# Gate and up projections of a ConvFFN by Strassen's seven products, in a hybrid decoder step on one core

## The chip, the cores and the metric

The kernel runs on one core of a Trainium2 chip. The metric is the device time of one execution in microseconds; three runs before the change took 1549.66, 1551.98 and 1552.0 us, median 1551.98. Engines are named as in the profile: PE is TensorE (matmul), PEld its weight loads, DVE is VectorE, ACT ScalarE, POOL GpSimd, SP SyncE, from which all transfers are issued.

## What is computed

The reference is one inference step of a two-layer decoder trunk for 512 prompt tokens and 8 sequences of 8 sample tokens, all in float32, with D_MODEL 1024 and D_FF 2816. Layer 0 mixes tokens by a convolution module beside windowed attention, layer 1 by a Mamba-2 mixer. After each mixer stands the part that is changed:

```python
def conv_ffn(h, hist, w_gate, w_up, conv_w, conv_b, w_down):
    gate = h @ w_gate
    padded = jnp.concatenate([hist, gate], axis=1)
    gc = causal_dwconv(padded, conv_w, conv_b)          # width 3
    y = (jax.nn.silu(gc) * (h @ w_up)) @ w_down
    return y, padded[:, -(FFN_CONV_WIDTH - 1):]
...
        fp, f1 = conv_ffn(rmsnorm(xp, norm_ffn[layer]), ...)
        xp = xp + fp
```

Here h is `x * rsqrt(mean(x^2) + eps) * g`. The last two gate rows of each sequence are outputs too.

## The kernel before

**Layout.** Activations lie transposed: channels on the 128 partitions, the 576 tokens (512 + 64) along the free axis, in two halves of 288 (`HALF`). x is eight tiles of 128x576. A projection's weights come as tiles of 128 output channels, 128x1024: eight blocks of 128x128, one for each 128 input channels.

**Three matmuls per product.** To keep float32 accuracy with the faster fp32r matmuls, each operand is split into a rounded high part and the rest. `weights` (L163, L164) does so for a weight tile (ACT copies the high part, DVE subtracts), `split` (L193, L194) for activations, and `mm3` (L173 to L175) issues high x high, high x low and low x high into one PSUM bank. A tile and half thus takes 8 x 3 = 24 matmuls of 128x288 with 24 weight loads.

**Norm.** With `early` set, as for both FFNs, `norm_tile` makes h as x times the gain as soon as a tile of x is final, and the matmuls run on that; the factor rs (one over the root of the mean square, from `rstd`, L202 to L220) is applied afterwards to the projections' sums (L329, L333, L334 for the gate, L347 for the up side). Without `early`, as for the Mamba layer (`norm_o`), `norm_half` scales h by rs first (L261) and splits it, and the matmuls wait for that.

**The FFN stage** (`ffn`). There are 22 gate and 22 up tiles of 128 channels. Three gate tiles go first (`lead`), then up tile f and gate tile f + 3 in turn. A gate tile's sums are written to `gbuf`, the history is put in front (POOL, L327, L328), the width-3 convolution runs on DVE (L339, L341 twice), SiLU on ACT (L344, L345). An up tile's sums are multiplied with that (L354) and split into a pair y. The down projection runs in three parts (`PARTS`, of 8, 7 and 7 tiles f), each as soon as its tiles are there: `out_proj` takes eight output tiles m in two halves, and `add_x` (L288) adds each sum to x on DVE. The last part of the first FFN also makes the next layer's norm.

**Order and buffers.** A scheduler at build time orders each engine's instructions by readiness in its own model, with the order of the program as priority; `keep_in_program_order` pins a matmul behind what was issued before it. On the chip each engine takes its queue in order. Raw weights have three buffers (`wr`), split ones three pairs (`wh`, `wl`). PSUM has eight banks: four in turn for projections (`mm`), four for the rest (`aux`). Other tiles come from a list of 48 + 11 slots in SBUF (`S`, `free`), first freed, first used again.

Of the kernel before, what the change touches and what calls it, by code (L numbers as in the profile page):

```python
# [23 lines left out]
PARTS = ((0, 8), (8, 15), (15, 22))  # L24
# [25 lines left out]

class Builder:
    NSLOT = 48
    EXTRA = 11

    def __init__(self, nc, tc, d, stack):
# [9 lines left out]
        self.used = {}  # L65

# [25 lines left out]
    def pm(self):  # L92
        return self.ps("mm", "mm")

# [140 lines left out]
    def norm_begin(self, gname, early):  # L235
        self.gname, self.early = gname, early
        self.ssq, self.rs = self.S("ssq"), self.S("rs")
        self.h = [self.pair("h") for _ in range(8)]
        self.hf = []
# [12 lines left out]
    def norm_half(self, half):  # L252
# [3 lines left out]
        if not self.early:  # L256
            for k in range(8):
# [5 lines left out]
                self.split(t[:, sl], self.h[k], sl)  # L263
# [3 lines left out]
    def norm_end(self):  # L267
        self.free(self.rs, self.h)
# [43 lines left out]
    def ffn(self, l, next_norm):  # L312
        nc, d = self.nc, self.d
        hist, so = self.S("fhist", NF * 16), self.S("fso", NF * 16)
# [4 lines left out]
        rs = self.rs  # L319
        bt = lambda ap: ap.rearrange("p (b t) -> p b t", t=8)  # L320

        def gate_evac(f):
            def go(half, p):
                if half == 0:
                    g = gbuf[f] = self.S("gbuf", 594)
                    gs = g[:, 514:594].rearrange("p (b c) -> p b c", c=10)
                    nc.gpsimd.memset(g[:, 0:2], 0.0)  # L327
                    nc.gpsimd.tensor_copy(gs[:, :, 0:2], hist[:, f * 16:f * 16 + 16].rearrange("p (b c) -> p b c", c=2))  # L328
                    nc.vector.tensor_tensor(g[:, 2:290], p[:, :HB], rs[:, :HB], op=MUL)  # L329
                    return  # L330
                g = gbuf.pop(f)
                gs = g[:, 514:594].rearrange("p (b c) -> p b c", c=10)
                nc.vector.tensor_tensor(g[:, 290:514], p[:, 0:224], rs[:, HB:NP], op=MUL)  # L333
                nc.vector.tensor_tensor(gs[:, :, 2:10], bt(p[:, 224:288]), bt(rs[:, NP:]), op=MUL)  # L334
                nc.gpsimd.tensor_copy(so[:, f * 16:f * 16 + 16].rearrange("p (b c) -> p b c", c=2), gs[:, :, 8:10])
                nc.gpsimd.tensor_copy(po[:, f * 2:f * 2 + 2], g[:, 512:514])  # L336
                cv = self.S("gconv", 594)
                w = lambda k: self.pv(f"fw{l}", f * 3 + k)
                nc.vector.tensor_scalar(cv[:, :592], g[:, 0:592], w(0), None, op0=MUL)  # L339
                for k in (1, 2):  # L340
                    nc.vector.scalar_tensor_tensor(cv[:, :592], g[:, k:592 + k], w(k), cv[:, :592], op0=MUL, op1=ADD)  # L341
                sl = sl_of[f] = self.S("gsilu")
                b = self.pv(f"fb{l}", f)
                nc.scalar.activation(sl[:, :NP], cv[:, :NP], AF.Silu, bias=b)  # L344
                nc.scalar.activation(bt(sl[:, NP:]), cv[:, 514:594].rearrange("p (b c) -> p b c", c=10)[:, :, 0:8],  # L345
                                     AF.Silu, bias=b)
                nc.vector.tensor_tensor(sl, sl, rs, op=MUL)  # L347
                self.free(g, cv)
            return go

        def up_evac(f):
            def go(half, p):
                sl = sl_of[f]
                nc.vector.tensor_tensor(sl[:, HALF[half]], p[:, :HB], sl[:, HALF[half]], op=MUL)  # L354
                if half == 1:
                    y_of[f] = self.pair("y")
                    self.split(sl, y_of[f])
                    self.free(sl_of.pop(f))
            return go
# [1147 lines left out]
```

## Time and profile before

| | |
|---|---|
| median of three runs | 1551.98 us (1549.66 to 1552.0) |
| span of the profiled execution | 1551.3 us |
| its time outside the span, against the median | 0.7 us |
| matmuls in the span | 11635 |
| first FFN, 217 to 630 us | 413.0 us, DVE busy 221.56, POOL 15.92 |
| second FFN, 1129.5 us to the end | 421.8 us, DVE busy 217.79, POOL 15.38 |

How to read the lines of the profile. A window's row gives from:to, its length, then the busy time of PE, PEld, DVE, ACT and POOL with the number of instructions, then the granted share of the TensorE clock, the busy share of the DMA engines and GB/s. A row of a group gives line, engine, operation, the tile written <- the tiles read, shapes and count, then busy us and the mean ns of one, then the idle time before them and what ended it. A row of one line's instructions gives the shortest, median and longest ns. A row of the timeline gives start and length in us, the instruction, how many were merged, and in brackets the idle time before it with what ended it.

### The profile page before, as it was taken

The numbers are of one execution on the slowest core, as the hardware profiler recorded it, in microseconds if no ns is written. First come the engines' busy times: TensorE is split into PE (matmuls) and PEld (weight loads), VectorE is DVE, ScalarE is ACT, GpSimd is POOL, SyncE is SP. The second block draws the span as 40 slices with busy tenths as digits, with TensorE's granted clock in tenths as the row PEclk, the third lists the DMA queues.
The fourth block names the chain that finished last, engine by engine and source line by source line (L and its number), as shares of the span: only waits on it lengthen the run. The fifth ranks groups of instructions, "written<-read, shape, count | busy, mean of one in ns | idle before, by whom it ended". The sixth has DMA issues, their size and how long they took to land.

```text
span 1551.3 us, 28549 instructions
## 1 busy us (share of the span) xinstructions
PE 1520.5 (98%) x11635; PEld 1449.8 (93%) x11635; DVE 1018.5 (66%) x1805; ACT 649.3 (42%) x1232; POOL 154.7 (10%) x365
## 2 busy tenths in 40 slices
PE   8999999999999999999999999999999999999999
PEld 7977799999999999898988988998999999999999
DVE  7969887553555464678896786777976644663552
ACT  6356553221222222486855654646632222321220
POOL 0036001000000000011211112102010000000000
PEclk9999999999999999999999999999999999999999
DMA  8515223222222222136245245245222222223222
GB/s 239 136 42 131 85 70 98 86 86 85 83 77 78 92 82 85 55 104 202 71 148 180 83 115 185 72 125 173 87 84 85 91 83 82 82 73 92 82 87 75
DMA packets 69938, 157.80 MB, mean 102 GB/s; under 512 B 19871, under 2 KB 24607, under 8 KB 69807
## 3 DMA queue, kind: packets, MB, share of 16 engines
q1 hardware_dynamic: 69806, 155.97, 33.2%
q8 instruction: 92, 1.51, 0.4%
q14 instruction: 40, 0.32, 0.1%
HBM read 140.73 MB, written 15.21 MB: 101 GB/s over the span
## 4 chain that ended last, share of the span: by engine, by line
PE 88%; DVE 5%; ACT 4%; DMA 2%; issue 1%; SPq 0%; ACTq 0%; DVEq 0%
PE mm L173 27%; PE mm L175 27%; PE mm L174 26%; DMA acb<-acd 2%; PE yp L1148 1%; DVE wl L164 1%; ACT acb L1116 1%; PE mm L594 1%; ACT wh L163 1%; PE pst L1081 1%; PE pt L1063 1%; ACT sm L661 1%; PE py L1133 1%; PE pst L1200 1%; DMA out_ssm_s<-h 1%
## 5 line engine op out<-in xcount | busy, mean ns | idle before, releaser
L173 PE MATMUL mm<-hh,wh 128*128 128x288 f32 x2272 | 677.8, 299 | 6.8 <-ACT wh L163 5.5
L174 PE MATMUL mm<-hl,wh 128*128 128x288 f32 x2272 | 673.9, 297 | 0.7 <-DVE hl L389 0.4
L175 PE MATMUL mm<-hh,wl 128*128 128x288 f32 x2272 | 673.3, 297 | 0.5 <-DVE wl L164 0.4
L163 ACT ACTIVATE wh<-wr 128x1024 fp32r<-128x1024 f32 (+2 forms) x215 | 223.3, 1039 | 544.6 <-PE mm L174 275.1
L173 PEld LDWEIGHTS mm<-hh,wh 128*128 128x128 f32 x2272 | 428.3, 189 | 16.0 <-ACT wh L163 6.0
L174 PEld LDWEIGHTS mm<-hl,wh 128*128 128x128 f32 x2272 | 429.0, 189 | 4.8 <-issue 1.8
L175 PEld LDWEIGHTS mm<-hh,wl 128*128 128x128 f32 x2272 | 428.7, 189 | 3.2 <-issue 1.4
L164 DVE TENSOR_TENSOR wl<-wr,wh 128x1024 fp32r<-128x1024 f32 (+2 forms) x215 | 258.6, 1204 | 73.0 <-ACT wh L163 71.4
L173 PE MATMUL mm<-yh,wh 128*128 128x288 f32 x960 | 285.9, 298 | 1.5 <-DVE x L288 1.4
L175 PE MATMUL mm<-yh,wl 128*128 128x288 f32 x960 | 284.2, 297 | 1.3 <-DVE wl L164 1.3
L174 PE MATMUL mm<-yl,wh 128*128 128x288 f32 x960 | 285.3, 297 | 0.0
L173 PEld LDWEIGHTS mm<-yh,wh 128*128 128x128 f32 x960 | 181.1, 189 | 5.7 <-DVE x L288 2.5
L175 PEld LDWEIGHTS mm<-yh,wl 128*128 128x128 f32 x960 | 181.1, 189 | 2.4 <-DVE wl L164 1.6
L174 PEld LDWEIGHTS mm<-yl,wh 128*128 128x128 f32 x960 | 181.2, 189 | 1.5 <-issue 1.0
L288 DVE TENSOR_TENSOR x<-x,mm 128x288 f32<-128x288 f32 x192 | 84.9, 449 | 143.0 <-PE mm L175 142.8
L333 DVE TENSOR_TENSOR gbuf<-mm,rs 128x224 f32<-128x224 f32 x44 | 17.2, 391 | 108.6 <-PE mm L175 108.6
L344 ACT ACTIVATE gsilu<-gconv,par 128x512 f32<-128x512 f32 x44 | 31.8, 724 | 115.1 <-DVE gconv L341 115.1
L341 DVE SCALAR_TENSOR_TENSOR gconv<-gbuf,par,gconv 128x592 f32<-128x592 f32 x88 | 73.1, 831 | 1.5
L354 DVE TENSOR_TENSOR gsilu<-mm,gsilu 128x288 f32<-128x288 f32 x88 | 40.0, 454 | 50.5 <-PE mm L175 50.5
L880 DVE SCALAR_TENSOR_TENSOR cconv<-cbuf,par,cconv 128x600 f32<-128x600 f32 x72 | 59.6, 838 | 10.1 <-ACT cconv L878 9.5
L336 POOL COPY fpo<-gbuf 128x2 f32<-128x2 f32 x44 | 12.4, 281 | 476.0 <-DVE gbuf L333 476.0
L1116 ACT ACTIVATE acb<-acb,ac 128x128 f32<-128x128 f32 x128 | 41.4, 390 | 35.6 <-DMA acb<-acd 25.0
(322 smaller groups left out, 1593.6 us busy)
## 6 DMA issues: line engine op xcount, KB each, us to landing
wr<-in_w_gate SPq DMA_DIRECT2D x44, 512.0 KB, 3.5
wr<-in_w_up SPq DMA_DIRECT2D x44, 512.0 KB, 3.5
wr<-in_w_in_o SPq DMA_DIRECT2D x40, 512.0 KB, 3.6
wr<-in_w_down SPq DMA_DIRECT2D x32, 448.0 KB, 3.3
wr<-in_w_down SPq DMA_DIRECT2D x16, 512.0 KB, 3.5
h<-in_h SPq DMA_DIRECT2D x32, 256.0 KB, 3.1
acb<-acd SPq DMA_DIRECT2D x32, 256.0 KB, 4.2
out_ssm_s<-h SPq DMA_DIRECT2D x32, 256.0 KB, 2.6
```

The costliest lines, as they stand in the source:

```text
L163: nc.scalar.activation(hi[:, a:b], raw[:, a:b], AF.Copy)
L164: nc.vector.tensor_tensor(lo[:, a:b], raw[:, a:b], hi[:, a:b].bitcast(F32), op=SUB)
L173: nc.tensor.matmul(out, hi[:, ws], xh[:, sl], start=i == 0, stop=False)
L174: nc.tensor.matmul(out, hi[:, ws], xl[:, sl], start=False, stop=False)
L175: nc.tensor.matmul(out, lo[:, ws], xh[:, sl], start=False, stop=i == n - 1)
L288: nc.vector.tensor_tensor(self.x[m][:, sl], self.x[m][:, sl], p[:, :HB], op=ADD)
L333: nc.vector.tensor_tensor(g[:, 290:514], p[:, 0:224], rs[:, HB:NP], op=MUL)
L341: nc.vector.scalar_tensor_tensor(cv[:, :592], g[:, k:592 + k], w(k), cv[:, :592], op0=MUL, op1=ADD)
L344: nc.scalar.activation(sl[:, :NP], cv[:, :NP], AF.Silu, bias=b)
L354: nc.vector.tensor_tensor(sl[:, HALF[half]], p[:, :HB], sl[:, HALF[half]], op=MUL)
L880: nc.vector.scalar_tensor_tensor(cv[:, :600], g[:, k:600 + k], w(k), cv[:, :600], op0=MUL, op1=ADD)
L1116: nc.scalar.activation(acb[:, cs], acb[:, cs], AF.Relu, bias=ac[:, o:o + 1], scale=-1.0)
```

## The change

Two output tiles f and f + 1 of the gate or the up projection are computed together as a 2x2 block product: tiles f and f + 1 are the two rows of blocks, the two halves of the 1024 input channels the inner index, the two halves of the tokens the columns. In place of the eight quarter products of that block product the kernel makes Strassen's seven (in Winograd's form), each of 4 x 3 matmuls of the same shape as before. Four sums of weight blocks, s1 to s4, are made by POOL for each pair, and four differences of blocks of h, T1 to T4, once per layer. Since these are needed, h is scaled by rs beforehand (`early` is False). The first four gate tiles (`LEAD`) are computed as before, from the quarters of h.

The sums of the seven products are shared by three PSUM banks z, y and x that a pair holds. Where two results need a common partial sum, it is copied out (r) or added to r in SBUF (e, a) before further products are accumulated in the bank. The pairs are overlapped by hand: per turn, the new pair's product 1, the old one's 3 and 7, the new one's 2 and 5, the old one's 4, the new one's 6.

Besides, the first convolution tap goes from DVE to ACT, an up tile's product with the gate from DVE to POOL (after an addition on DVE), the down projection has five parts of 4, 4, 4, 4 and 6 tiles, PSUM banks are divided six to two, and there are six more slots in SBUF, for which the scratch space of dynamic DMA shrinks.

```diff
-PARTS = ((0, 8), (8, 15), (15, 22))
+LEAD = 4
+PARTS = ((0, 4), (4, 8), (8, 12), (12, 16), (16, 22))
...
+class Strassen:
...
+    def load(self):
+        b, nc = self.b, self.nc
+        low, up = b.weights_load(self.job.src[1], 1024), b.weights_load(self.job.src[0], 1024)
+        a11, a12, a21, a22 = up[:, 0:512], up[:, 512:1024], low[:, 0:512], low[:, 512:1024]
+        self.up, self.a22 = up, a22
+        s1, s2, s3, s4 = self.s = [b.S(f"st{i}", 512) for i in range(4)]
+        nc.gpsimd.tensor_tensor(s1, a21, a22, op=ADD)
+        nc.gpsimd.tensor_tensor(s2, s1, a11, op=SUB)
+        nc.gpsimd.tensor_tensor(s4, a12, s2, op=SUB)
+        nc.gpsimd.tensor_tensor(s3, a11, a21, op=SUB)
+        self.d = b.S("dh", 512, F32R), b.S("dl", 512, F32R)
+        self.split(a22, *self.d)
...
+    def alpha(self):
+        self.w1 = self.tiles()
+        self.split(self.up, *self.w1)
...
+    def beta(self):
+        self.w2 = self.two(self.s[0], self.s[1])
+    def gamma(self):
+        self.w3 = self.two(self.s[3], self.s[2])
+    def product(self, bank, w, col, q, first, last):
...
+        for k, t in enumerate(self.b.hq[q]):
+            ws = slice(col + k * P, col + k * P + P)
+            xh, xl = t[:, 0:HB], t[:, HB:T]
+            m = nc.tensor.matmul(out, hi[:, ws], xh, start=first and k == 0, stop=False, skip_group_check=skip)
+            if k == 0:
+                self.b.tc.keep_in_program_order(m)
+            nc.tensor.matmul(out, hi[:, ws], xl, start=False, stop=False, skip_group_check=skip)
+            nc.tensor.matmul(out, lo[:, ws], xh, start=False, stop=k == 3, skip_group_check=skip)
+    def p1(self):
+        self.z = self.b.hold("z")
+        self.product(self.z, self.w1, 0, "B11", True, False)
...
+        self.nc.scalar.activation(self.r, self.z[:, :HB], AF.Copy)
+    def p2(self):
+        self.product(self.z, self.w1, 512, "B21", False, True)
+        self.job.c11(self.z[:, :HB])
...
+    def p5(self):
...
+        self.product(self.y, self.w2, 0, "T1", True, False)
+        self.nc.vector.tensor_tensor(self.e, self.r, self.y[:, :HB], op=ADD)
+    def p6(self):
...
+        self.product(self.x, self.w2, 512, "T2", True, False)
+        self.nc.vector.tensor_tensor(self.a, self.r, self.x[:, :HB], op=ADD)
+    def p3(self):
+        self.product(self.y, self.w3, 0, "B22", False, True)
+        self.job.c12(self.a, self.y[:, :HB])
...
+    def p7(self):
+        self.product(self.x, self.w3, 512, "T3", False, False)
+        self.job.c22(self.e, self.x[:, :HB])
+    def p4(self):
+        self.product(self.x, self.d, 0, "T4", False, True)
+        self.job.c21(self.r, self.x[:, :HB])
...
+    EXTRA = 17
...
+    def combine(self):
+        nc, (a, b) = self.nc, HALF
+        hf = self.hf
+        for k in range(4):
+            u, v = hf[k], hf[k + 4]
+            nc.gpsimd.tensor_tensor(u[:, a], u[:, b], u[:, a], op=SUB)
+        self.quarter("T1", [t[:, a] for t in hf[:4]])
...
+        def gate_done(f):
...
+            nc.scalar.activation(cv[:, :592], g[:, 0:592], AF.Copy, scale=w(0))
+            for k in (1, 2):
+                nc.vector.scalar_tensor_tensor(cv[:, :592], g[:, k:592 + k], w(k), cv[:, :592], op0=MUL, op1=ADD)
...
+        class Gate:
...
+            def second(me, f, u, v):
+                g = gbuf[f]
+                nc.vector.tensor_tensor(g[:, 290:514], u[:, 0:224], v[:, 0:224], op=ADD)
+                nc.vector.tensor_tensor(samples(g)[:, :, 2:10], bt(u[:, 224:HB]), bt(v[:, 224:HB]), op=ADD)
+            def c12(me, u, v):
+                me.second(me.f, u, v)
+                gate_done(me.f)
+            def c22(me, u, v):
+                gate_open(me.f + 1)
+                me.second(me.f + 1, u, v)
...
+        class Up:
...
+            def part(me, f, half, u, v):
+                nc.vector.tensor_tensor(u, u, v, op=ADD)
+                s = sl_of[f][:, HALF[half]]
+                nc.gpsimd.tensor_tensor(s, s, u, op=MUL)
...
+        for job in todo + [None]:
+            new = Strassen(self, job) if job else None
+            if new:
+                new.load()
+                new.alpha()
+                new.p1()
+            if prev:
+                prev.gamma()
+                prev.p3()
+                prev.p7()
+            if new:
+                new.p2()
+                new.beta()
+                new.p5()
+            if prev:
+                prev.p4()
+            if new:
+                new.p6()
+            while due:
+                down(due.pop(0))
+            if prev and isinstance(prev.job, Up) and prev.job.f in ends:
+                due.append(ends[prev.job.f])
+            prev = new
...
-        self.norm_begin("norm_f0", True)
+        self.norm_begin("norm_f0", False, True)
...
-        self.norm_begin("norm_f1", True)
+        self.norm_begin("norm_f1", False, True)
...
-    nc = bacc.Bacc("TRN2", target_bir_lowering=False, num_devices=1)
+    nc = bacc.Bacc("TRN2", target_bir_lowering=False, num_devices=1, dynamic_dma_scratch_size=1024)
```

The list `todo` holds an up pair and a gate pair in turn, the gate four tiles ahead; a part of the down projection is put into `due` a turn after its last up pair and runs at the end of the turn that follows.

More of the change, by code (lines that the diff above doesn't have):

```diff
@@ L93, in pm, with hold, give @@
         return self.ps("mm", "mm")
+    def hold(self, name):
+        b = self.rings["mm"].pop(0)
+        t = self.pp.tile([P, 512], F32, tag=f"b{b}", bufs=1, name=name)
+        self.held[id(t)] = (b, t)
+        return t
+    def give(self, t):
+        self.rings["mm"].append(self.held.pop(id(t))[0])
     def pv(self, name, i=0, n=1):
@@ L262, in norm_half @@
                                                op0=MUL, op1=MUL)
-                self.split(t[:, sl], self.h[k], sl)
+                if not self.in_quarters:
+                    self.split(t[:, sl], self.h[k], sl)
+                elif k % 4 == 3:
+                    name = f"B{k // 4 + 1}{half + 1}"
+                    self.quarter(name, [h[:, sl] for h in self.hf[k - 3:k + 1]])
         if half == 1:
@@ L323, in go, with lead_evac @@
+        def lead_evac(f):
             def go(half, p):
                 if half == 0:
[L325 to L329, printed above, removed]
-                    return
@@ L331, in go @@
[L331 to L337, printed above, removed]
@@ L347, in go @@
-                nc.vector.tensor_tensor(sl, sl, rs, op=MUL)
-                self.free(g, cv)
-            return go
[L351 to L359, printed above, removed]
-        G = lambda f: (d["w_gate"][l, f], P, gate_evac(f))
@@ new lines, in ffn, with leads @@
+        lead = [(d["w_gate"][l, f], lead_evac(f)) for f in range(LEAD)]
+        parts = {half: [(t[:, :HB], t[:, HB:]) for q in ("B11", "B21") for t in self.hq[q[:2] + str(half + 1)]] for half in (0, 1)}
+        def leads(todo):
+            ws = [self.weights(src, 1024) for src, _ in todo]
+            for half in (0, 1):
+                for w, (_, evac) in zip(ws, todo):
+                    p = self.pm()
+                    self.mm3(p[:, :HB], w, range(8), parts[half], slice(0, HB))
+                    evac(half, p)
@@ L368, in ffn, with down @@
+        leads(lead[:3])
+        self.combine()
+        leads(lead[3:])
+        self.free(self.hq.pop("B12"))
+        def down(p):
+            a, b = PARTS[p]
             last = b == NF
@@ L378, in ffn @@
             self.free([y_of.pop(f) for f in range(a, b)])
+        todo = []
+        for f in range(0, NF, 2):
+            todo.append(Up(f))
+            if f + LEAD < NF:
+                todo.append(Gate(f + LEAD))
+        ends = {b - 2: p for p, (a, b) in enumerate(PARTS)}
+        prev, due = None, []
+        for job in todo + [None]:
[21 more added lines that the diff above has]
+            prev = new
+        while due:
+            down(due.pop(0))
     def mix0(self):
```

121 lines of the change are left out of this document (99 added, 22 removed).

## The prediction

> **What bounds the kernel now.** I read the page first: busy shares, then the chain of work that ended last, then the windows of the two FFN stages, then the groups by shape.
>
> ```profile
> span 1551.3 us, 28549 instructions
> PE 1520.5 (98%) x11635; PEld 1449.8 (93%) x11635; DVE 1018.5 (66%) x1805; ACT 649.3 (42%) x1232; POOL 154.7 (10%) x365
> PE 88%; DVE 5%; ACT 4%; DMA 2%; issue 1%; SPq 0%; ACTq 0%; DVEq 0%
> ```
> ```profile
> 300.00:340.00 40.00, 40.00 (x303) 40.00 (x302) 24.70 (x39) 11.36 (x16) 2.19 (x12) 1.00 0.27 80
> 217.00:630.00 413.00, 413.00 (x3113) 412.50 (x3112) 221.56 (x350) 109.82 (x153) 15.92 (x75) 1.00 0.28 84
> 1129.50:1551.30 421.80, 418.21 (x3161) 417.52 (x3160) 217.79 (x341) 103.36 (x136) 15.38 (x72) 1.00 0.27 84
> ```
>
> The first three lines say that TensorE is the bound: 98% busy, 88% of the last-ending chain. Busy PE alone can mislead since matmuls overlap, so the window from 300 to 340 us, the middle of the first FFN, is what I use: TensorE never paused, 303 matmuls started in 40.00 us, that is 0.132 us each, while VectorE had 24.70 us of work and POOL 2.19. The other two rows are the two FFN stages: 413 and 422 us, VectorE at 54% and 52%. So in this stage a matmul that is not issued is time saved, for as long as the other engines keep up. The median of the runs, 1551.98 us, is 0.7 us above the profiled span; I sum against 1552.
>
> **Matmuls removed.** Before, a layer's 44 gate and up tiles take 44 x 2 halves x 8 blocks x 3 = 2112 matmuls. After, four lead gate tiles stay as they were (192) and 40 tiles become 20 pairs, each of seven products of 4 x 3 matmuls, 20 x 84 = 1680. That is 240 fewer per layer, 480 in all; the down projections keep 22 x 8 x 2 x 3 = 1056. Shape and weight loads are those of the row above, so 480 x 0.132 = **63.4 us less**. A layer's TensorE work becomes 2928 x 0.132 = 386.5 us, a product 12 x 0.132 = 1.58 us, a pair 11.1 us.
>
> **What is added beside it.** These groups give the prices:
>
> ```profile
> L164 DVE TENSOR_TENSOR wl<-wr,wh 128x1024 fp32r<-128x1024 f32 x181 | 222.3, 1229 | 61.0 <-ACT wh L163 59.5 <-PE pyo L1170 1.5
> L1078 DVE TENSOR_TENSOR xde<-xdt,de 128x512 f32<-128x512 f32 x16 | 10.5, 677 | 0.0
> L341 DVE SCALAR_TENSOR_TENSOR gconv<-gbuf,par,gconv 128x592 f32<-128x592 f32 x88 | 73.1, 831 | 1.5
> L194 DVE TENSOR_TENSOR yl<-gsilu,yh 128x576 fp32r<-128x576 f32 x44 | 33.0, 751 | 0.0
> L354 DVE TENSOR_TENSOR gsilu<-mm,gsilu 128x288 f32<-128x288 f32 x88 | 40.0, 454 | 50.5 <-PE mm L175 50.5
> L333 DVE TENSOR_TENSOR gbuf<-mm,rs 128x224 f32<-128x224 f32 x44 | 17.2, 391 | 108.6 <-PE mm L175 108.6
> L334 DVE TENSOR_TENSOR gbuf<-mm,rs 128x64 f32<-128x64 f32 x44 | 9.4, 214 | 0.0
> L288 DVE TENSOR_TENSOR x<-x,mm 128x288 f32<-128x288 f32 x192 | 84.9, 449 | 143.0 <-PE mm L175 142.8
> L261 DVE SCALAR_TENSOR_TENSOR hf<-x,par,rs 128x288 f32<-128x288 f32 x16 | 7.5, 514 | 0.9 <-ACT rs L220 0.9
> L194 DVE TENSOR_TENSOR hl<-hf,hh 128x288 fp32r<-128x288 f32 x16 | 6.5, 453 | 1.8 <-ACT hh L193 1.8
> L164 DVE TENSOR_TENSOR wl<-wr,wh 128x896 fp32r<-128x896 f32 x32 | 34.9, 1092 | 11.9 <-ACT wh L163 11.9
> L1176 POOL TENSOR_TENSOR h<-h,cds 128x512 f32<-128x512 f32 x32 | 40.4, 1292 | 133.9 <-PE pyo L1170 133.9
> L163 ACT ACTIVATE wh<-wr 128x1024 fp32r<-128x1024 f32 x181 | 191.5, 1059 | 431.1 <-issue 215.3 <-PE mm L174 211.3 <-DMA h<-in_h 1.8
> L1117 ACT ACTIVATE acb<-acb 128x512 f32<-128x512 f32 x32 | 19.7, 622 | 0.4
> L193 ACT ACTIVATE hh<-hf 128x288 fp32r<-128x288 f32 x16 | 6.5, 439 | 4.7 <-DVE hf L261 4.7
> L878 ACT ACTIVATE cconv<-cbuf,par 128x600 f32<-128x600 f32 x24 | 19.1, 794 | 0.6
> ```
>
> VectorE, per pair. Weights: one 128x1024 split at 1.229 and five 128x512 ones (a22, s1, s2, s4, s3) at 0.677 (L1078, also two SBUF inputs of that size): 4.61 us against 2.46 for the two tiles before. The sums e and a after products 5 and 6: 2 x 0.454 = 0.91. A gate pair then has two split adds of 0.391 + 0.214, one of 0.454, and four taps of 0.831: 4.99; the first tap and the product with rs leave VectorE. An up pair has four operations of 0.454 and two splits of 0.751: 3.32. So a gate pair costs 10.5 us and an up pair 8.8.
>
> VectorE, per layer: 9 gate pairs 94.6, 11 up pairs 97.2, the leads' weights 4 x 1.229 = 4.9 and their taps 8 x 0.831 = 6.6, down weights 8 x (4 x 0.677 + 0.95, between the rows of 512 and 896) = 29.3, 80 additions to x at 0.449 = 35.9 (48 before, 32 of them new with five parts), h scaled 16 x (0.514 + 0.453) = 15.5, the three-quarter combinations 16 x 0.453 = 7.2. Sum **291 us of 386.5**, 75%, where it was 221.56 of 413.
>
> POOL, per layer: 80 weight sums of 128x512. L1176 is the one group of that shape, and its shortest is 1.037 us (below): 83 us. Then 33 products of the up pairs and 16 differences of h at 128x288, bounded by 9/16 of that (0.58) and the whole of it (1.04); no row has the shape, and I take 0.6 as the time scales with size on VectorE: 29 us. Together 112 us.
>
> ScalarE: 20 x (1.059 + 5 x 0.622) in place of 40 x 1.059 adds 41 us, 40 copies of 0.44 out of PSUM 18, 22 first taps of 0.794 17. With the 109.82 us of the window this is 186 of 386: off the path. DMA moves the same bytes; in the window it is 28% busy, so I cost it at nothing, and if a load came late it would be once per pair, the raw buffers still being three.
>
> **What VectorE and POOL cost each other.** POOL is nearly idle in the FFN now. Where it does work:
>
> ```profile
> L1176 POOL TENSOR_TENSOR h<-h,cds x32: 1037/1198/2061, 723.1 to 1065.9; 128x512 f32<-128x512 f32 x32
> L1153 DVE TENSOR_TENSOR xs<-xs,ea x16: 548/552/1214, 719.8 to 1079.9; 128x384 f32<-128x384 f32 x16
> L1118 DVE TENSOR_TENSOR acb<-acb,cbm x32: 676/691/1532, 709.0 to 1076.5; 128x512 f32<-128x512 f32 x32
> L1266 DVE TENSOR_TENSOR xs<-xs,zs x32: 443/450/1294, 740.4 to 1088.1; 128x288 f32<-128x288 f32 x32
> L1180 DVE TENSOR_TENSOR yo<-pyo,eax x8: 676/680/691, 724.2 to 1064.3; 128x512 f32<-128x512 f32 x8
> ```
> ```profile
> 736.85 5.04 POOL L1176 TENSOR_TENSOR h<-h,cds 128x512 f32<-128x512 f32 x4 [0.73 <-PE pyo L1170]
> 737.10 1.21 DVE L1153 TENSOR_TENSOR xs<-xs,ea 128x384 f32<-128x384 f32 x1
> 738.23 0.68 DVE L1180 TENSOR_TENSOR yo<-pyo,eax 128x512 f32<-128x512 f32 x1
> 738.83 0.93 DVE L1118 TENSOR_TENSOR acb<-acb,cbm 128x512 f32<-128x512 f32 x1
> 740.37 2.20 DVE L1266 TENSOR_TENSOR xs<-xs,zs 128x288 f32<-128x288 f32 x3 [0.61 <-ACT zs L1262]
> ```
>
> While four POOL multiplications ran, L1153 took 1.21 us against its median of 0.552, L1118 0.93 against 0.691, three L1266 2.20 against 3 x 0.450; L1180, which reads PSUM, kept its 0.68. So an operation with two SBUF inputs stands still while POOL reads, and POOL while it runs (2061 against 1037). VectorE lost 0.66 + 0.24 + 0.85 = 1.75 us in 5.04, **0.35 us per us of POOL**. [...]
>
> After the change about three quarters of a pair's VectorE time has two SBUF inputs, so I take 0.4, with 0.14 and 1 as bounds for the range (0.14 is the first step alone, 0.66 over 5.04, rounded up; 1 is full turns). A layer's VectorE then needs 291 + 0.4 x 112 = 336 of 386 us: TensorE stays the bound on average. But the down parts come in lumps. Between them lie four pairs, two of each kind: TensorE 4 x 11.1 = 44.4 us, VectorE 38.7, POOL 16 x 1.04 + 6 x 0.6 = 20.2, so 38.7 + 8.1 = 46.8. A down part of four tiles (192 matmuls, 25.3 us, with 12.6 us of VectorE) lets VectorE run ahead, but only by what the three weight buffers hold: the next first split and the previous gamma pair and half, 1.23 + 0.68 + 1.35 = 3.3 us at the least. That covers the 2.4 missing. So throughput alone costs little; order costs more.
>
> **The new waits.** Product 7 leaves its sum in the bank to which product 4 adds, and c22 must read it in between. Only the new pair's products 2 and 5 lie there: 3.17 us. In that time VectorE, which takes its queue in order, may have in front of c22: the rest of c12 (0.605), two taps (1.66) and beta's two splits (1.35), and then c22 itself (0.605): 4.2 us for a gate pair, about 1.0 too late, 1.2 with a POOL operation in between. Behind c22 wait product 4, product 6 and all that follows on TensorE. For an up pair it is 0.454 + 0.751 + 1.35 + 0.454 = 3.0, and 0.2 too late with POOL. On POOL the four sums, 4.2 us, may stand ahead of an up pair's products; these feed y, which only the next down part reads, more than a pair later. Per layer 9 x 1.2 + 11 x 0.2 = 13 us. The bound below is nothing, if the queue's order puts c22 ahead of the taps; above, the full-turn rival.
>
> **The openings.** The factor rs was applied after the matmul; now h is scaled first and TensorE waits for it. The present opening, and the stage change at 650 us, where L261 already scales h first:
>
> ```profile
> 215.54 0.81 DVE L288 TENSOR_TENSOR x<-x,mm 128x288 f32<-128x288 f32 x2
> 216.67 0.41 ACT L220 ACTIVATE rs<-pr 128x288 f32<-128x288 f32 x1
> 649.31 0.40 PE L218 MATMUL pr<-dg,l 128*128 128x288 f32 x1 [1.17 <-DVE dg L214]
> 650.21 0.40 PE L173 MATMUL mm<-hh,wh 128*128 128x288 f32 x1 [0.50 <-ACT rs L220]
> 647.00:650.50 3.50, 1.83 (x12) 1.51 (x13) 1.93 (x5) 1.28 (x4) 0.00 (x0) 1.00 0.39 137
> 652.40:655.80 3.40, 3.40 (x20) 3.40 (x20) 2.36 (x6) 0.96 (x3) 0.00 (x0) 0.71 0.00 0
> ```
>
> Now rs is ready at 217.1, when the last sums of the output projection are being added; after the change the first block of h comes 0.51 + 0.44 + 0.45 = 1.4 us later with nothing else for TensorE, so 1.4 idle. At 649 a pause of 1.17 and 0.50 us was followed by a granted clock of 0.71 over 3.4 us, which costs 1.0 us there. [...] I take 3 us per opening, 6 in all, between 2 x 1.4 and 2 x 4.1 (1.4 with the 1.17, 0.50 and 1.0 of 649 on top). Up to the first product 5, TensorE then has 216 x 0.132 = 28.5 us of work, VectorE 16 x 0.967 (scaling) + 1.8 (T1) + 5.0 (taps of three leads) + 1.2 (the fourth's weights) + 3.3 (the first pair's splits) = 26.8, and 16 x 0.6 x 0.4 = 3.8 beside POOL's differences: 30.6, so 2 us short, 4 in all. The first FFN's end loses 3 x 3 x 0.132 = 1.2 us of cover, since its last part has 18 matmuls per sum where it had 21: 1. Two PSUM banks instead of four for other sums I cost at nothing: only the two of the rs calculation live there.
>
> **The sum.** 1552 - 63.4 + 26 (the waits of both layers) + 6 + 4 + 1 = **1526 us**.
>
> **Rivals.** First, *everything hidden*: if c22 is ahead of the taps in the queue, the 26 go and the openings shrink: 1552 - 63.4 + 6 + 1 = 1496, up to 1506. For it: VectorE at 87% of TensorE on average, every deadline over 3 us. Against: the four-pair stretches have no slack.
>
> Second, *slower: VectorE and POOL in turns*. If each of POOL's operations stops VectorE for its whole length, a layer needs 291 + 112 + POOL's present small copies, 16 in the window: 419 us of turns, against the 413 and 421.8 of today's windows (mean 417), and 6 + 4 at the openings: 1552 + 2 x (419 - 417) + 10 = 1566, and more where the down parts don't lend their slack (ten stretches of 38.7 + 20.2 - 44.4 - 3.3 = 11.2 too long would be 112: 1552 - 63.4 + 112 + 11 = 1612). It decides when the loss per us of POOL passes some 0.72: a stretch then costs 38.7 + 14.6 - 3.3 = 50.0 us, 5.6 over TensorE's 44.4, and ten stretches eat the 63.4 - 7. For it: three quarters of VectorE's time is of the kind that stands still. Against: 0.35 measured, and the PSUM operations and fixed parts run beside POOL. [...]
>
> Third, *clock*: if the waits cluster as at 649, each clustered wait costs a further 1.0 us of low clock; 40 pairs, 1526 + 40 = 1566. For it: the fall at 649. Against: a wait of 1.2 in 11 us leaves TensorE far busier than the 1.83 of 3.5. Fourth, *nothing left*: waits of 1.4 us per pair, 40 x 1.4 = 56, eat the gain: 1552.
>
> **Chances.** Forecast, 1507 to 1548: 0.58. All hidden: 0.16. Nothing left, 1549 to 1555: 0.05. In turns: 0.17. Clock: 0.04. About 0.2%, 3 us, is what a measurement of this kernel can tell from no change. So faster 0.74, same 0.05, slower 0.21. The range, 1497 to 1560, leaves out the upper part of the slower cases and little below; the forecast's own is 1507 to 1548.
>
> **What would show it.** Right: 480 fewer matmuls at 0.132 us in quiet windows; TensorE idle some 13 us per FFN before product 4, ended by the c22 add, and more in gate than in up pairs; two-input VectorE operations up to 1 us longer beside POOL, PSUM ones unchanged; VectorE about 87% busy between 240 and 600 us; 2 to 3 us idle at each FFN's start. Wrong: idle before products 1 or 5, ended by a weight split (then VectorE or POOL is the bound and the second rival holds), waits for a weight load, or matmuls of another length.

## The result, and the profile after

After the change the kernel takes 1614.86 us (median of 4 runs, 1614.17 to 1617.95) where the runs beside it of the kernel before take 1551.99: a ratio of 1.0408, with a 95% interval of 1.0393 to 1.0423. The prediction was 1526, so it has the wrong sign, and the time lies 89 us from it.

The first lines of the page of the kernel after: span, busy shares, and the chain that ended last.

```profile
span 1612.8 us, 28657 instructions
PE 1495.8 (93%) x11155; PEld 1405.5 (87%) x11155; DVE 1202.0 (75%) x2075; ACT 798.0 (49%) x1588; POOL 503.0 (31%) x623
PE 55%; DVE 24%; ACT 6%; POOL 5%; issue 5%; DMA 4%; SPq 0%; POOLq 0%; DVEq 0%; ACTq 0%
```

The matmuls are 11635 - 11155 = 480 fewer, as said. But TensorE's share of the chain fell from 88% to 55%, and VectorE, ScalarE and POOL now hold 35% of it, although none of them is more than 75% busy. That is the picture of engines that wait for each other.

Where the time went shows in the windows of the kernel after: each FFN's opening (lead tiles), then its pairs and down parts up to the last product, for both layers, and the 40 us that the prediction used.

```profile
217.00:268.00 51.00, 34.98 (x202) 31.54 (x203) 46.30 (x69) 27.75 (x65) 34.56 (x32) 0.83 0.16 51
268.00:632.30 364.30, 335.96 (x2453) 329.26 (x2453) 256.52 (x400) 149.34 (x259) 156.45 (x178) 0.99 0.26 81
300.00:340.00 40.00, 37.77 (x280) 37.27 (x281) 27.30 (x51) 17.49 (x32) 10.04 (x18) 1.00 0.20 58
1161.50:1208.40 46.90, 31.91 (x166) 28.43 (x164) 39.29 (x53) 23.44 (x54) 33.53 (x37) 0.75 0.16 53
1208.40:1570.20 361.80, 335.37 (x2454) 328.90 (x2453) 253.96 (x400) 149.54 (x259) 156.76 (x174) 0.99 0.25 80
```

At 0.132 us a matmul the openings lose 51.00 - 202 x 0.132 = 24.3 and 46.90 - 166 x 0.132 = 25.0 us, the pairs 364.30 - 2453 x 0.132 = 40.5 and 361.80 - 2454 x 0.132 = 37.9: 128 us against the 63.4 saved, which gives the result within 2 us. The prediction had 11 for openings and ends and 26 for the pairs. In 300:340 there are 280 matmuls where there were 303.

What TensorE waits for in the pairs shows in the groups by shape of the kernel after (last column: idle time just before, and what ended it), and what those engines wait for in turn in two rows of its view of waits (who waited <- for whom: us in total, times, longest us).

```profile
L104 PE MATMUL x<-hqT,dh 128*128 128x288 f32 x160 | 50.3, 314 | 26.4 <-DVE st L534 16.2 <-DVE gbuf L511 10.2
L104 PE MATMUL x<-hqT,wh 128*128 128x288 f32 x320 | 97.7, 305 | 20.2 <-DVE st L130 20.2
L104 PE MATMUL y<-hqB,wh 128*128 128x288 f32 x160 | 48.4, 302 | 5.3 <-DVE st L125 4.8
```
```profile
ACT yh L301 <- POOL gsilu L536: 189.8, 44, 6.8
DVE yl L302 <- ACT yh L301: 109.1, 44, 5.6
```

Product 4 (x from the weights dh) waits 26.4 us for c22, 16.2 of it for an up pair's (L534) and 10.2 for a gate pair's (L511). Product 7 waits 20.2 us for the sum a that VectorE makes after product 6. Both wait for VectorE. With product 3's 5.3 us these are 51.9 of the 78.4 us that the two pair windows lose; the rest is not attributed to single waits here. And VectorE stood still for 109.1 us, waiting for ScalarE's copy yh of a finished up tile, which stood still for 189.8 us, waiting for POOL's product L536. One such place in the timeline of the kernel after:

```profile
360.16 1.29 POOL L67 TENSOR_TENSOR st<-wr 128x512 f32<-128x512 f32 x1 [1.99 <-DMA wr<-in_w_gate]
361.41 0.81 POOL L536 TENSOR_TENSOR gsilu<-gsilu,st 128x288 f32<-128x288 f32 x1
362.24 0.68 ACT L301 ACTIVATE yh<-gsilu 128x576 fp32r<-128x576 f32 x1 [6.10 <-POOL gsilu L536]
362.83 1.04 ACT L73 ACTIVATE wh<-wr 128x1024 fp32r<-128x1024 f32 x1
362.96 0.76 DVE L302 TENSOR_TENSOR yl<-gsilu,yh 128x576 fp32r<-128x576 f32 x1 [3.88 <-ACT yh L301]
363.63 0.45 DVE L534 TENSOR_TENSOR st<-st,x 128x288 f32<-128x288 f32 x1
364.14 0.40 PE L104 MATMUL x<-hqT,dh 128*128 128x288 f32 x1 [2.08 <-DVE st L534]
```

Read from the bottom: product 4 waited 2.08 us for c22's addition (L534). That needed only product 7, but stood in VectorE's queue behind yl (L302), which waited 3.88 us for yh (L301), which waited 6.10 us for the product (L536), which stood on POOL behind a weight sum (L67) that itself had waited for its load. Nobody needed y there. Behind yh on ScalarE stood the next weights' copy (L73) as well.

### The profile page after: what moved, and what is told of

Read it like the earlier page. It is cut to its first block, busy times and chain, and to the rows that moved or that the text cites. A ratio compares the mean times of both kernels' runs of the same rounds, so it can differ in the third digit from the quotient of the medians.

```text
span 1612.8 us, 28657 instructions
## 1 busy us (share of the span) xinstructions
PE 1495.8 (93%) x11155; PEld 1405.5 (87%) x11155; DVE 1202.0 (75%) x2075; ACT 798.0 (49%) x1588; POOL 503.0 (31%) x623
## 4 chain that ended last, share of the span: by engine, by line
PE 55%; DVE 24%; ACT 6%; POOL 5%; issue 5%; DMA 4%; SPq 0%; POOLq 0%; DVEq 0%; ACTq 0%
PE mm L281 14%; PE mm L283 14%; PE mm L282 14%; DVE wl L74 7%; DVE gconv L482 2%; POOL gsilu L536 2%; DMA wr<-in_w_gate 2%; DVE hf L399 2%; DVE wl L272 2%; ACT yh L301 2%; POOL st L67 1%; DVE dl L74 1%; DVE hqT L356 1%; PE x L104 1%; DVE hqB L356 1%
## 5 line engine op out<-in xcount | busy, mean ns | idle before, releaser
L281 PE MATMUL mm<-hh,wh 128*128 128x288 f32 x864 | 262.1, 305 | 7.4 <-ACT wh L271 5.3
L282 PE MATMUL mm<-hl,wh 128*128 128x288 f32 x864 | 259.1, 301 | 0.5 <-DVE hl L302 0.2
L283 PE MATMUL mm<-hh,wl 128*128 128x288 f32 x864 | 257.6, 299 | 1.8 <-DVE wl L272 1.8
L271 ACT ACTIVATE wh<-wr 128x1024 fp32r<-128x1024 f32 (+3 forms) x167 | 144.7, 867 | 192.9 <-PE mm L282 170.1
L272 DVE TENSOR_TENSOR wl<-wr,wh 128x1024 fp32r<-128x1024 f32 (+3 forms) x167 | 167.1, 1006 | 45.5 <-ACT wh L271 42.2
L281 PEld LDWEIGHTS mm<-hh,wh 128*128 128x128 f32 x864 | 163.9, 190 | 15.3 <-ACT wh L271 5.6
L282 PEld LDWEIGHTS mm<-hl,wh 128*128 128x128 f32 x864 | 164.3, 190 | 5.0 <-issue 1.7
L283 PEld LDWEIGHTS mm<-hh,wl 128*128 128x128 f32 x864 | 164.3, 190 | 4.2 <-DVE wl L272 2.2
L74 DVE TENSOR_TENSOR wl<-st,wh 128x512 fp32r<-128x512 f32 x160 | 150.1, 971 | 2.8 <-ACT wh L73 2.4
L301 ACT ACTIVATE yh<-gsilu 128x576 fp32r<-128x576 f32 x44 | 30.1, 685 | 189.8 <-POOL gsilu L536 189.8
L104 PE MATMUL x<-hqT,wh 128*128 128x288 f32 x320 | 97.7, 305 | 20.2 <-DVE st L130 20.2
L302 DVE TENSOR_TENSOR yl<-gsilu,yh 128x576 fp32r<-128x576 f32 x44 | 34.0, 774 | 109.1 <-ACT yh L301 109.1
L73 ACT ACTIVATE wh<-st 128x512 fp32r<-128x512 f32 x160 | 93.9, 618 | 21.8 <-PE mm L282 21.2
```

Source lines behind the costliest of these rows:

```text
L73: nc.scalar.activation(hi, src, AF.Copy)
L74: nc.vector.tensor_tensor(lo, src, hi.bitcast(F32), op=SUB)
L104: m = nc.tensor.matmul(out, hi[:, ws], xh, start=first and k == 0, stop=False, skip_group_check=skip)
L271: nc.scalar.activation(hi[:, a:b], raw[:, a:b], AF.Copy)
L272: nc.vector.tensor_tensor(lo[:, a:b], raw[:, a:b], hi[:, a:b].bitcast(F32), op=SUB)
L281: nc.tensor.matmul(out, hi[:, ws], xh[:, sl], start=i == 0, stop=False)
```

## The experiments

Theory A, *order*: yh and yl stand in in-order queues before POOL has made their input, and hold what TensorE needs. Theory B, *turns*: POOL's new operations stop VectorE for so long that VectorE's time is short, the prediction's second rival. For the openings: either the order of their steps, or VectorE's load as such. Medians are in us; each ratio is to runs of the kernel before on the same chip.

**The product to VectorE.**

```diff
-                nc.gpsimd.tensor_tensor(s, s, u, op=MUL)
+                nc.vector.tensor_tensor(s, s, u, op=MUL)
```

> Only the product of an up tile's half with its gate (33 per layer, 128x288) goes from POOL to VectorE. Theory A (order): the product stands on POOL behind the four weight sums, ScalarE's copy yh waits for it (189.8 us of waiting named in the changed kernel's waits), VectorE's yl waits for the copy (109.1 us), and both in-order queues hold the weight splits and adds that TensorE needs; so nearly all of the idle time ahead of products 7 and 3 and a good part of that ahead of product 4 goes: 1614.9 - 50 = 1565 us, between 1555 and 1585. Theory B (VectorE and POOL in turns, the sum of both counts): POOL loses 33 x 0.94 = 31 us a layer, VectorE gains 33 x 0.45 = 15, so at most 16 us a layer, 1614.9 - 32 = 1583, and less where the loss is 0.45 us of VectorE per us of POOL: 31 x 0.45 = 14 saved against 15 added, 1615.

Measured: 1578.07, ratio 1.018 (1.0142 to 1.0218). VectorE is 1253.7 - 1202.0 = 51.7 us busier, and the kernel 37 us faster. That is inside A's range, 13 us short of its likeliest value, but the interval also holds B's 1583 (a ratio of 1.020), so the time alone does not decide. The waits say more: the idle time before product 7 is gone, and yl waits 13.6 us for yh where it waited 109.1. Yet 17.5 us are left before product 4, all of it ended by a gate pair's c22 (L511), while yh on ScalarE still waits 143.4 us for the product, now VectorE's.

**The copies of y one turn later in the program.**

```diff
-                me.close(me.f)
+                late.append(lambda: me.close(me.f))
...
+            for f in ready if new else ready + late:
+                f()
```

> The copies of y into two parts (yh on ScalarE, yl on VectorE) are issued one turn later, after product 6; POOL, the sums and the product stay as they are, and each engine does the same work. Theory A (order): ScalarE and VectorE no longer stand before a product that POOL has not begun, and 30 to 60 of the some 80 us of idle TensorE in the two layers' pairs go: 1555 to 1585, 1570 likeliest. Theory B (turns): the same work and the same overlap, so 1615 within 5 us.

Measured: 1598.03, ratio 1.0309 (1.0279 to 1.0339). 17 us, between the two. The waits view shows why: yh still waited 133.7 us for L536. In the order that the scheduler made at build time the copies stood ahead again. So this run didn't settle it.

**No weight sums.**

```diff
-        nc.gpsimd.tensor_tensor(s1, a21, a22, op=ADD)
...
+        self.from_ = [a21, a11, a11, a12]
```

> Leaves out the four weight sums of each pair on POOL (160 of 128x512 in the two layers) and splits raw weight blocks in their place, so what it computes is not the reference's; TensorE, ScalarE and VectorE have the same operations. Both theories let the 80 us of idle TensorE in the pairs go, and the first pair's sums no longer slow the scaling of h in the openings (some 10 us each): 1614.9 - 80 - 20 = 1515. It sets the bound that the other runs are read against: if moving the copies or the product alone comes within 20 us of it, order was the cause; if they do not move and this does, the sums' hold on VectorE was. Above 1580 both are wrong, and the waits are TensorE's or ScalarE's own.

Measured: 1538.98, ratio 0.9933 (0.9908 to 0.9958), 76 us less than the changed kernel, nearly all of it in the pairs. Raw weight blocks are split in place of the sums, so the outputs are not the reference's, but the other engines have the same operations. The opening, 209 matmuls in the same 51 us, lost 23.4 still, so the 20 us expected there did not come, and the first pair's sums were not what the opening lost by. The busy row of its page, against the one above, prices the sums:

```profile
PE 1474.3 (96%) x11155; PEld 1397.4 (91%) x11155; DVE 1131.6 (74%) x2075; ACT 801.1 (52%) x1588; POOL 257.7 (17%) x463
```

With the same 2075 instructions VectorE is 70.4 us less busy without them.

**The opening, all lead tiles first, the first pairs' loads held back.**

```diff
         leads(lead[:3])
-        self.combine()
         leads(lead[3:])
+        self.combine()
...
+                    with self.tc.issue_after(self.last_diff):
+                        new.load()
```

> Only the openings of the two FFNs: the four lead tiles run before h is combined into sums, and the first two pairs' weight loads and sums begin only after POOL's last difference of h. Theory A (the opening loses because POOL's first sums run beside VectorE's scaling of h, and because the fourth lead tile's weight split stands behind the combinations): of the 25.6 and 21.5 us lost there some 15 each go, 1614.9 - 30 = 1585, between 1570 and 1595. Rival: the openings are short of VectorE time as such (46.30 us busy in the 51 us), so what the first pair gains the first products lose, 1615 within 8.

Measured: 1612.05, ratio 1.0399 (1.0369 to 1.0429). The time is the rival's: idle time before the lead tiles fell from 31.2 to 18.9 us, and before products 1 and 2 (tile z) it rose from 2.8 to 17.7. But the edit itself puts the first pair's weights behind POOL's last difference of h and so behind VectorE's splits of T1 to T4, so this run does not tell load from order.

**The copies of y held behind in the queues themselves.** `issue_after` queues what its block issues behind the given instruction of the same engine; `hi` is ScalarE's last copy for beta, `add` VectorE's sum a.

```diff
+            if new:
+                with self.tc.issue_after(new.hi), self.tc.issue_after(new.add):
+                    for f in ready:
+                        f()
```

> As the late close, but the order on the chip is forced: the copies yh and yl of an up pair are queued on ScalarE behind the next pair's last copy of s2 and on VectorE behind its sum a, in each engine's own queue, since the scheduler at build time had put them ahead again (yh still waited 133.7 us for POOL's product). The work of every engine stays the same. Theory A (order: a copy that waits for POOL's product holds the weight splits behind it): the waits of yh fall under 40 us and 35 to 60 us of idle TensorE go against the changed kernel's 1614.9, 1565, between 1550 and 1580. Theory B (VectorE and POOL in turns): no change beyond the 17 us of the late close, 1595 to 1600.

Measured: 1552.3, ratio 1.0012 (0.9984 to 1.0039): 62 us less by order alone. Its busy row, two of its groups, and the window of its first FFN's pairs:

```profile
PE 1478.8 (95%) x11155; PEld 1396.9 (90%) x11155; DVE 1237.8 (80%) x2075; ACT 803.8 (52%) x1588; POOL 539.6 (35%) x623
```
```profile
L74 DVE TENSOR_TENSOR wl<-st,wh 128x512 fp32r<-128x512 f32 x160 | 173.4, 1120 | 2.4 <-ACT wh L73 2.4
L105 PE MATMUL x<-hqT,dh 128*128 128x288 f32 x160 | 47.4, 296 | 0.0
```
```profile
268.00:597.80 329.80, 328.17 (x2455) 325.81 (x2454) 271.99 (x401) 152.08 (x258) 174.72 (x179) 1.00 0.29 90
```

The same instructions as in the changed kernel, VectorE 36 us and POOL 37 us *busier* by the records, a weight split at 1120 ns where it was 971, so they collide more; yet the pairs lose 329.80 - 2455 x 0.132 = 5.7 us in place of 40.5, and product 4 waits for nothing. Theory B can't give that. Yh's waits for POOL fell to 25.6 us. The edit moves yh and yl together, so it doesn't tell what ScalarE's queue and what VectorE's cost.

**The sums to VectorE, the product still on POOL.**

```diff
-        nc.gpsimd.tensor_tensor(s1, a21, a22, op=ADD)
+        nc.vector.tensor_tensor(s1, a21, a22, op=ADD)
...
```

> The four weight sums of each pair go from POOL to VectorE, the product stays on POOL. VectorE gains 160 x 0.68 = 109 us and loses the 70 us that the sums cost it (1202.0 against 1131.6 us busy without them), so it is some 39 us busier. Theory A (the product stood behind the sums on POOL): its wait is short now, as with the product on VectorE: 1575, between 1560 and 1590. Theory B (the time lost is VectorE's time): VectorE has more to do than before, 1615 or more, up to 1640.

Measured: 1549.97, ratio 0.9998 (0.9979 to 1.0018), 65 us less and below A's range. VectorE is 24.5 us busier (1226.5), so theory B falls here too. Taking the sums out of POOL's queue brought 65 us and taking the product out 37; in both the product no longer stood behind the sums. Why the second brought less was not tested; its yh still waited for VectorE's product, and the sums still ran beside VectorE.

**Sums and product to VectorE.** Both edits above.

> Sums and product both on VectorE; POOL keeps only the differences of h and its small copies. VectorE gains 109 + 30 us and loses the holds of the sums (70) and of the product (some 20), so it is about 50 us busier, as with the product alone on VectorE (1253.7). Theory A (order, no wait of one engine for POOL's backlog): 1560 to 1580, like the product alone, and the idle time before products 7 and 3 stays gone. Rival (VectorE is then the bound of a stretch): four pairs need 2 x 13.2 + 2 x 12.9 = 52 us of VectorE against 44.4 of TensorE and 3.3 of lead, 4.5 us in each of ten stretches, so idle time before products 1 and 5 and 1590 to 1615.

Measured: 1533.88, ratio 0.9896 (0.9868 to 0.9925), faster than either kernel, better than A's range. Its windows, opening and pairs of the first FFN:

```profile
217.00:268.00 51.00, 34.72 (x208) 32.11 (x209) 46.39 (x77) 27.88 (x66) 27.98 (x26) 0.83 0.18 60
268.00:593.80 325.80, 324.85 (x2448) 324.50 (x2447) 274.87 (x504) 151.16 (x259) 23.61 (x71) 1.00 0.29 89
```

The pairs lose 325.80 - 2448 x 0.132 = 2.7 us with VectorE busy 274.87 of 325.80, 84%: the rival that a stretch of four pairs needs more of VectorE than there is falls too. The opening still loses 51.00 - 208 x 0.132 = 23.5.

**The sums of h later, for the opening.** All lead tiles, then the first pair; T1 ahead of product 5, T2 of product 6, T3 and T4 after it.

```diff
-        leads(lead[:3])
-        self.combine()
-        leads(lead[3:])
+        leads(lead)
+        combine = self.combine()
...
+                next(combine, None)
                 new.beta()
```

> Only the openings: all four lead tiles first, then the first pair's weights and products 1 and 2; the sums of h are made one at a time, T1 ahead of product 5, T2 ahead of product 6, T3 and T4 after it. Theory A (the splits of T2 to T4, alternating with POOL's differences at about 1.0 us each, stand ahead of the weights that TensorE needs): of the 25.6 and 21.5 us lost in the openings 10 to 15 each go, 1615 - 25 = 1590, between 1580 and 1600. Rival (VectorE has too much to do in the opening whatever the order): 1612 within 5, as with all four leads first.

Measured: 1612.21, ratio 1.0402 (1.035 to 1.0454): 3 us, the rival. In the first 51 us 237 matmuls ran in place of 202, 4.6 us' worth, and the pairs gave most of that back.

**The same with sums and product on VectorE**, where the pairs have nothing to give back; the lead tiles go in groups of three and one. The lines shown are against the edit before.

```diff
-        leads(lead)
+        leads(lead[:3])
+        leads(lead[3:])
```

> Sums and product on VectorE as in the 1533.9 us run, and the four lead tiles ahead of the sums of h, which are made one at a time for the first pair's products. With the pairs no longer idle, nearly all that is lost now lies in the two openings, 23.4 and 24.0 us. Theory A (the fourth lead tile's weights stand behind the splits of T1 to T4 in both in-order queues, 7.2 us, and the clock falls after it): that gap and some 2 us of low clock go in both layers, 1534 - 18 = 1516, between 1510 and 1525. Rival (VectorE has too much to do there in any order, as the same edit gained only 3 us with the sums on POOL): 1531 within 4.

Measured: 1523.85, ratio 0.9823 (0.9805 to 0.984): 28 us faster than before and 91 than the changed kernel. Of the 18 us expected 10 came, which is inside theory A's range, at its slow end.

**Six lead tiles**, with the order as it was, and with the sums of h behind them; both with sums and product on VectorE.

```diff
-LEAD = 4
+LEAD = 6
```

> Sums and product on VectorE, and six lead gate tiles in place of four, the order as it was (three, the sums of h, three). Per layer one pair less by seven products: 12 matmuls more, 1.6 us, and 12.7 us more work for TensorE in the opening against some 6 us of VectorE. If the opening is short of VectorE time, this lends it 6 us a layer: 1534 + 3 - 12 = 1525. If the gap comes from the order alone, the splits of T1 to T4 still stand ahead of the fourth tile's weights and the 7.2 us stay: 1534 + 3 = 1537.

> Sums and product on VectorE, six lead tiles, and the sums of h behind them one at a time. If order is the cause in the opening, as the four-tile version of this edit or less, 1516 + 3 - 5; if VectorE's time is, this is the only one of the three that covers it. 1514, between 1507 and 1530.

Measured: 1539.06, ratio 0.992 (0.99 to 0.9941), and 1526.83, ratio 0.9838 (0.9819 to 0.9857). More matmuls in the opening bring nothing: with the old order the pause before the fourth tile stays, as the order theory said, and with the new one the intervals with four and six overlap. In the first FFN of that last kernel 279 matmuls ran from 217 to 268 us, where the kernel with four had 237, but with the next window, to 300 us, the counts are 480 and 478.

**The differences of h to VectorE**, on top of sums and product, and on top of the later sums of h.

```diff
-            nc.gpsimd.tensor_tensor(u[:, a], u[:, b], u[:, a], op=SUB)
+            nc.vector.tensor_tensor(u[:, a], u[:, b], u[:, a], op=SUB)
...
```

> Sums and product on VectorE, and the 16 differences of h too; POOL has no operation with two SBUF inputs left in the FFN. In the opening the splits of T1 to T4 and POOL's differences go in turns, 0.98 us for one of each, where alone a split takes 0.45 and a difference on VectorE 0.45. If the two exclude each other, VectorE alone is no slower, 0.9 us for both: 1532 within 4. [...]

> As the 1523.9 us kernel with the differences of h on VectorE as well. If VectorE and POOL go in turns there, VectorE alone is about as fast, 1524 within 4; if waiting for POOL in ScalarE's queue (the high copies of T1 to T4 stand there for POOL's differences) is part of what is left, 1518.

Measured: 1532.09, ratio 0.9872 (0.9849 to 0.9894), and 1525.83, ratio 0.9819 (0.9793 to 0.9846): no change either time. In the opening a split and a difference take 0.99 us on the two engines (last section) and 0.90 on VectorE alone, so nothing is won by sharing the work.

**h scaled by x in place of rs**, on top of the 1523.85 kernel.

```diff
-self.pv(self.gname, k), self.rs[:, sl],
+self.pv(self.gname, k),
+                                               self.x[k][:, sl] if self.in_quarters else self.rs[:, sl],
```

> As the 1523.9 us kernel (sums and product on VectorE, lead tiles ahead of the sums of h), but h of the two FFNs is scaled by x itself in place of rs: the same instruction with the same number of SBUF inputs, not the reference's values, and free of the wait for the norm. 18.6 and 17.8 us are still lost in its two openings, and the prediction had put 3 us of each down to the wait for the scaled h. Theory A (the chain norm, rs, scaling, split, with its half clock afterwards, is the larger part of what is left): the first pause of 3.1 us, the one of 2 us at the second half and most of the low clock go, 1524 - 20 = 1504, between 1496 and 1512. Rival (VectorE's load: 48.1 us busy of 51): the pauses move behind the leads, 1524 - 5 = 1519, between 1514 and 1524.

Measured: 1520.24, ratio 0.979 (0.9773 to 0.9808): 3.6 us by the medians, inside the rival's range, and the intervals of the two ratios overlap a little. This kernel leaves rs out of h, so its values are not the reference's. It is not a clean test, since the matmul that makes rs is still in TensorE's queue and waited there, as its timeline shows:

```profile
224.96 0.61 PE L326 MATMUL pr<-dg,l 128*128 128x288 f32 x1 [3.27 <-DVE dg L322]
```

## Why the prediction was wrong, point by point

**Matmuls removed: right.** 480, still 0.132 us where nothing waits; the value of 63.4 us was there to be had. The time came out 89 us above the forecast because the pairs lost 78.4 us in place of 26 and the openings 49.3 in place of 10.

**The step that failed** is this sentence: "On POOL the four sums, 4.2 us, may stand ahead of an up pair's products; these feed y, which only the next down part reads, more than a pair later." The data are needed late, that is true. But two instructions of other engines already stand in their queues to fetch them, yh and yl, and both queues waited there, yh 189.8 us in all and yl 109.1, although nobody needed y yet. The prediction had named the queue behind c22, not the one behind yl. Holding the two copies back brings 62 us, most of the 78.4 that the pairs lost: theory A is shown by the held copies, and again, with another remedy, by the sums moved off POOL.

**The new waits: the number right by luck.** 26 us were forecast before product 4, and 26.4 measured. But of the 26 the forecast had 2 x 9 x 1.2 = 21.6 in gate pairs and 2 x 11 x 0.2 = 4.4 in up pairs; measured were 10.2 and 16.2. The forecast had c22 late behind c12, taps and splits. With the copies held, c12 and taps still stand ahead of a gate pair's c22 and splits ahead of an up pair's, and product 4 waits 0.0. So those alone did not make c22 late in the changed kernel: the stop at yh and yl ahead of them did. That they can add to it the first run suggests, where yl hardly waited and a gate pair's c22 was late ten times, 17.5 us in all. The 20.2 us before product 7 weren't forecast at all; they too went with the copies held (1.0 left).

**VectorE's load and what POOL costs it: right in size.** Taken were 0.4 us of VectorE per us of POOL (0.35 measured before). The 160 sums cost VectorE 70.4 us and took POOL these times in the kernel after:

```profile
L66 POOL TENSOR_TENSOR st<-wr,st 128x512 f32<-128x512 f32 x40 | 60.7, 1517 | 16.6 <-DVE yl L302 15.9
L65 POOL TENSOR_TENSOR st<-st,wr 128x512 f32<-128x512 f32 x40 | 60.1, 1504 | 23.3 <-DMA wr<-in_w_gate 14.1 <-DMA wr<-in_w_up 4.4 <-PE mm L283 2.2
L64 POOL TENSOR_TENSOR st<-wr 128x512 f32<-128x512 f32 x40 | 58.2, 1455 | 138.2 <-DMA wr<-in_w_gate 79.8 <-PE mm L283 24.7 <-DVE yl L302 14.3
L67 POOL TENSOR_TENSOR st<-wr 128x512 f32<-128x512 f32 x40 | 56.2, 1405 | 29.6 <-DMA wr<-in_w_gate 23.2 <-DMA wr<-in_w_up 4.0 <-PE mm L283 2.4
L536 POOL TENSOR_TENSOR gsilu<-gsilu,st 128x288 f32<-128x288 f32 x66 | 61.4, 937 | 82.2 <-DVE st L534 82.2
```

70.4 / 235.2 = 0.30. VectorE was forecast 87% busy; in the first FFN's pairs it was 256.52 of 364.30 us, 70%, and with the copies held 271.99 of 329.80, 82%. POOL's own prices were low: about 1.47 us a sum where 1.04 was taken, 0.94 a product where 0.6 was. Most of that is POOL's own length: the sum at 360.16 in the timeline took 1.29 and the product at 361.41 took 0.81 with VectorE idle. That made POOL's backlog longer.

**The openings: the step mis-sized** was "I take 3 us per opening" and "2 us short"; 10 us were forecast for both, 49 are lost. The groups of VectorE in the kernel after, from 217 to 268 us:

```profile
L399 DVE SCALAR_TENSOR_TENSOR hf<-x,par,rs 128x288 f32<-128x288 f32 x16 | 14.1, 942 | 0.9 <-ACT rs L328 0.9
L356 DVE TENSOR_TENSOR hqT<-hf,hqT 128x288 fp32r<-128x288 f32 x16 | 9.9, 677 | 0.0
L356 DVE TENSOR_TENSOR hqB<-hf,hqB 128x288 fp32r<-128x288 f32 x16 | 9.8, 673 | 0.0
```

The scaling took 14.1 us for the 8.2 taken, the splits of B 9.8 for 7.2, both beside POOL, and all 16 splits of T were done at once, 9.9 us, where 4 were counted (1.8), because program order put them ahead of the fourth lead tile's weights. That is 5.9 + 2.6 + 8.1 = 16.6 us, 12.8 more than the 3.8 that the forecast had for POOL; with its 30.6 it makes 43.4 of the 46.30 busy in the window, and small operations of the norm are about the rest. The clock has a part in the 24.3 us lost too; it was granted at 0.83 over this window. At half clock, from 222.7 to 226.1, 239.8 to 243.2 and 259.5 to 263.7 us, 45 matmuls took 11.0 us where 5.9 would do at 0.132, an estimated 5 us where the forecast had 1.0. The longest single pause stands in the timeline of the kernel after:

```profile
259.53 0.61 PE L281 MATMUL mm<-hqB,wh 128*128 128x288 f32 x1 [7.23 <-ACT wh L271]
```

Putting these splits later gained 10 us of 47, making the differences on VectorE nothing, leaving out rs some 4 as far as that run can tell. What remains in the 1523.85 kernel goes with VectorE busy there nearly all the time:

```profile
217.00:268.00 51.00, 37.88 (x237) 35.19 (x238) 48.10 (x80) 32.08 (x75) 27.34 (x30) 0.90 0.16 52
```

That is 51.00 - 237 x 0.132 = 19.7 us lost, with VectorE busy 48.10; that its load is the cause is argued from that share. No run that takes load away from VectorE there, and nothing else, was made, and the six lead tiles, which gave TensorE more to do there, brought nothing by 300 us; so this part stays open.

**The rivals.** "In turns" gave 1566 and up to 1612, close to the result, and by a mechanism that the held copies refute: the collisions are there, in many operations, but VectorE, 82% busy in the pairs of that run, has the slack to take them. That the result lies near its upper value is chance. "All hidden" (1496 to 1506) is what the pairs did once the order was mended, and only the openings kept the time above. "Clock" needed a low clock in the pairs; there it was 0.99, and the low clock came in the openings, at 0.83 and 0.75. The 1 us for the end of the first FFN wasn't measured by itself.

## What to carry to other kernels

When an operation moves to a slower or busier engine, don't ask only when its result is needed: ask which instructions of other engines already stand in a queue to take it, and what stands behind those. A copy that is not urgent can stop the engine that everybody waits for (62 us came back here when two such copies were held back): queue it behind the urgent work, or keep its producer out of any backlog. And a wait forecast to the microsecond (26 against 26.4) is no proof of its cause: move only the order and see whether it goes.

## What the runs showed of the hardware

POOL and VectorE hold each other up, here in the opening of the kernel after:

```profile
247.13 5.96 DVE L356 TENSOR_TENSOR hqT<-hf,hqT 128x288 fp32r<-128x288 f32 x6
```
```profile
246.85 2.00 POOL L369 TENSOR_TENSOR hf<-hf 128x288 f32<-128x288 f32 x2
248.81 1.02 POOL L374 TENSOR_TENSOR hf<-hf 128x288 f32<-128x288 f32 x1
249.80 1.02 POOL L369 TENSOR_TENSOR hf<-hf 128x288 f32<-128x288 f32 x1
250.78 2.00 POOL L374 TENSOR_TENSOR hf<-hf 128x288 f32<-128x288 f32 x2
```

Six splits and six differences take 6 us side by side, 0.99 for one of each; a split alone is 0.45 (453 ns for the 16 of L194 in the kernel before). A POOL product of this size took 0.81 with VectorE idle (361.41 us above), so if a difference takes as long, strict turns would make 1.26, an estimate: the two slow each other, but not by the whole length of each. Moving the differences to VectorE, where they take 0.45 too, costs nothing, as the two runs show. The trace shows that the two collide, and doesn't show that one stands still for the other's whole instruction: in the kernel before, L1153 began 0.25 us after the POOL product at 736.85 us, which took 1.05, and ended 0.41 us after that one's end, where its median is 0.55, so about 0.14 us of its work, an estimate, was done beside POOL. Over the 160 sums VectorE lost 0.30 us per us of POOL.

The clock fell after a pause of 2.20 us. Two windows of the kernel after (the last three numbers: granted clock, DMA share, GB/s) and the pause ahead of the first of them:

```profile
239.80:243.20 3.40, 3.40 (x14) 3.40 (x15) 3.40 (x6) 1.66 (x5) 2.12 (x3) 0.50 0.00 0
256.80:263.70 6.90, 4.08 (x15) 3.73 (x16) 6.90 (x13) 5.72 (x12) 5.72 (x4) 0.51 0.21 72
```
```profile
238.82 0.40 PE L282 MATMUL mm<-hqB,wh 128*128 128x288 f32 x1 [2.20 <-DVE hqB L356]
```

A pause of 2.20 us was followed by half the clock for 3.40 us, 14 matmuls where 26 fit at 0.132; in the 3.40 us before it, from 236.4 to 239.8, TensorE had been busy 0.89 us. And half the clock for 6.90 us began within the pause of 7.23 us that ended at 259.53.
